# Recurrence gates in four corners of the array, attention heads two by two, and a softmax one projection ahead of its values

## The chip, the cores and the metric

The kernel runs on one core of one Trainium2 chip. The metric is the device time of one execution in microseconds (us). The engines are TensorE (PE; its weight loads are listed as PEld), VectorE (DVE), ScalarE (ACT), GpSimd (POOL) and SyncE (SP). PE writes its results into PSUM banks; ACT and DVE read them from there. DMAs are issued from SP's queue (weights), POOL's and ACT's.

## What is computed

Two blocks in a row on 256 tokens of width 1024, all in 32-bit floats. The first has two layers: dilated attention with spatial gating, then a convolution with stick-breaking attention, each followed by a mixture of 16 experts. The second block has one gated linear recurrence and one neighbourhood attention. What the change touches, cut to its core:

```python
# first block, layer 0: 8 heads of 64, causal, with a relative bias
s = q[h] @ k[h].T * 64**-0.5 + bias[h];  o[h] = softmax(s) @ v[h]

# second block: recurrence over 1024 channels in 16 blocks of 64, both directions
r = sigmoid(block_diag(x, w_r) + b_r)          # gates: 64 x 64 per block
i = sigmoid(block_diag(x, w_i) + b_i)
a = exp(-8 * r * softplus(-lam));  u = sqrt(1 - a*a) * (i * x)
h = associative_scan(a, u)                      # forward and backward

# second block: 16 heads of 64 on a grid of 4 x 64, with a relative bias
o[h] = softmax(q[h] @ k[h].T * 64**-0.5 + nb[h]) @ v[h]
merged = sigmoid(ga) * (y_a @ w_pa) + sigmoid(gb) * ((o * silu(zb)) @ w_pb)
```

## The kernel before

Activations lie with channels on the 128 partitions and the 256 tokens along the free axis, in 8 chunks (`KD`). Every weight tile is 1 MB, loaded by SP into a ring of buffers (`load`, L198); a slot comes free when its projection has used it (`free`). A projection (`proj_ws`, L460) splits a weight tile into a high part `wh` (`split`, L449: ACT at L454, or DVE at L452 where `DVS` says so) and a low part `wl` (DVE, L457). It then does 48 matmuls of 128x128 by 256 columns (L471 to L473), and hands the sums to an evacuation function.

The source order is not the order on the engines. A planner of the language takes the instructions of each engine by their place in the source as a priority, and gives out the first one whose inputs and buffers are ready by its own model of time. The engines then run their queues in that fixed order. So a matmul can stand well ahead of its place in the source, between those of a projection. PSUM banks are taken by `bank(tag, name)`; each of the tags A, B, C and D has two.

**Modulation fill.** `ada_rows` (L347, L351) multiplies one weight tile with a vector, in four column groups of 32. `some_fill` puts such tiles between other work.

**First attention** (L1144 to L1172). For each of four head pairs `hp` and each head `s` in it: two score matmuls into a bank C (L1149, L1150), maximum and bias on DVE (L1153 to L1155), exponentials on ACT (L1157, L1158), normalisation on DVE (L1159 to L1161), three transposes on PE into a bank B (L1164), a copy on ACT (L1166), two value matmuls (L1167, L1168) into the pair's bank D. Then the pair is split into high and low parts (L1169, L1170) and two fill tiles follow.

**Recurrence** (`lru`, L1404 to L1441). It is a generator whose steps stand between the projections `b2_x` 0 to 11 and the first `b2_z`, two after each (`some_lru(LRU)`, L1472, L1482). It takes the 8 chunks of the convolved input `xc` in two halves (`q`) of four. Per chunk: a weight DMA `lw` on POOL's queue (L1412, two buffers), eight gate matmuls of 64 rows by 64 columns on 256 tokens (L1418: two directions `d`, two gates `g`, two blocks `b`), and four sigmoids (L1419, L1420). Block `b` reads partitions 64b to 64b+63 and writes the same partitions. A direction's two gates share a bank B. After the four chunks of a half come exponentials and tanh on ACT, a square root on ACT, and scans on DVE (L1437 to L1440) into `ys`. `ys` is read by the evacuations of `b2_z` 4 to 7.

**zb.** `b2_z` 0 to 3 are evacuated into `zb` (L1481), allocated at L1401, used by the second attention at L1534.

**Second attention** (`attend`, L1505 to L1536). For each of eight pairs: a bias DMA `nb` on POOL's queue (two buffers); per head two score matmuls into a bank C (L1516), maximum and bias on DVE (L1518, L1519), exponentials (L1521), normalisation (L1522 to L1524), four transposes into a bank B (L1528), a copy on ACT (L1530), two value matmuls into the pair's bank D (L1532); then the product with `zb` and the split (L1534 to L1536). The probabilities `sb` have two buffers (pool `lk2`). The loop at L1538 does projection `b2_z` 8+i and then `attend(i)`.

## Time and profile before

| what | us |
|---|---|
| median of three runs | 1213.07 (1211.43 to 1214.85) |
| the profiled execution | 1206.12 |
| its span, first to last instruction | 1204.1 |
| PE busy in the span | 1111.1 (92%) |
| DVE busy | 644.1 (53%) |
| ACT busy | 416.2 (35%) |
| POOL busy | 14.1 (1%) |

The first attention lies at about 108 to 141 us of the span, the first block ends at about 870, the recurrence stands between projections from 884 to 982, and the second attention ends at 1131. The shares are means over stages with different limits, so the rows below are taken stage by stage. Overlapped matmuls are drawn with their full length, so counts and starts of PE rows say more than their busy time.

### The profile page before, as it was taken

Reading aid. Unit: us, or ns where it says so; the run is one execution under the profiler, and the core shown is the slowest. Engines: PE = TensorE matmul, PEld = TensorE weight load, DVE = VectorE, ACT = ScalarE, POOL = GpSimd, SP = SyncE. Lnnn points to the kernel's source line nnn. Section 1 sums busy time; section 2 is a strip of 40 time slices with the busy share of each in tenths; the row PEclk is TensorE's granted clock in tenths of the full one; section 3 lists DMA queues with packets and bytes.
Section 4 is the critical chain, followed back from the end, with each engine's and each line's share of the span. In section 5 each row is a group of like instructions: output and inputs, shape, how many; then the busy total and the mean of one; then the engine's idle time right before and its main releaser. Section 6 shows DMA issues by size and latency. Waiting matters only on the chain. (4 is left out here: it accounts for less than half of the span.)

```text
span 1204.1 us, 20780 instructions
## 1 busy us (share of the span) xinstructions
PE 1111.1 (92%) x8168; PEld 794.1 (66%) x8172; DVE 644.1 (53%) x1488; ACT 416.2 (35%) x802; POOL 14.1 (1%) x32
## 2 busy tenths in 40 slices
PE   5899998999999989999898998899899999999996
PEld 3786575555555469868555554554578889788895
DVE  4665454333333359787623332232598787656665
ACT  2434331111111153365311121111446636445543
POOL 0000000000000000000000000000000000000000
PEclk9899889999999999999999999999899999999998
DMA  9999768999999988568858999998344445544340
GB/s 382 411 401 411 289 255 318 416 410 416 416 418 418 397 309 308 220 247 324 325 207 339 405 420 383 397 409 320 133 175 160 152 142 197 176 153 145 125 173 35
DMA packets 50551, 353.36 MB, mean 293 GB/s; under 512 B 5904, under 2 KB 6288, under 8 KB 8784
## 3 DMA queue, kind: packets, MB, share of 16 engines
q1 hardware_dynamic: 48544, 344.59, 72.9%
q0 software_dynamic: 1552, 6.03, 1.5%
q8 instruction: 104, 1.70, 0.6%
q14 instruction: 63, 0.52, 0.1%
q10 hardware_dynamic: 288, 0.52, 0.1%
HBM read 350.07 MB, written 1.05 MB: 292 GB/s over the span
## 5 line engine op out<-in xcount | busy, mean ns | idle before, releaser
L816 PE MATMUL gu<-ring,xg 128*64 128x256 f32 x1024 | 237.3, 385 | 2.0 <-issue 2.0
L815 PE MATMUL gu<-ring,xg 128*64 128x256 f32 x1024 | 236.9, 385 | 1.7 <-issue 1.6
L471 PE MATMUL pw<-xh,wh 128*128 128x256 f32 x736 | 212.2, 290 | 7.9 <-ACT wh L454 2.6
L457 DVE TENSOR_TENSOR wl<-ring,wh 128x1024 fp32r<-128x1024 f32 x144 | 175.2, 1222 | 71.9 <-ACT wh L454 68.0
L473 PE MATMUL pw<-xh,wl 128*128 128x256 f32 x736 | 210.6, 287 | 2.2 <-DVE wl L457 2.2
L472 PE MATMUL pw<-xl,wh 128*128 128x256 f32 x736 | 209.6, 286 | 0.0
L815 PEld LDWEIGHTS gu<-ring,xg 128*64 128x64 f32 x1024 | 138.1, 138 | 68.6 <-issue 8.4
L454 ACT ACTIVATE wh<-ring 128x1024 fp32r<-128x1024 f32 x114 | 120.0, 1058 | 151.0 <-PE pw L472 80.5
L471 PEld LDWEIGHTS pw<-xh,wh 128*128 128x128 f32 x736 | 141.8, 193 | 19.5 <-issue 11.3
L816 PEld LDWEIGHTS gu<-ring,xg 128*64 128x64 f32 x1024 | 138.2, 138 | 18.9 <-issue 10.3
L473 PEld LDWEIGHTS pw<-xh,wl 128*128 128x128 f32 x736 | 142.2, 193 | 6.0 <-DVE wl L457 3.3
L472 PEld LDWEIGHTS pw<-xl,wh 128*128 128x128 f32 x736 | 142.3, 193 | 1.4 <-DVE mf L1079 0.4
L841 PE MATMUL y<-ring,ht 128*64 128x512 f32 (+1 forms) x576 | 128.1, 563 | 6.6 <-DVE ht L835 5.0
L827 DVE SCALAR_TENSOR_TENSOR hd<-hs,gc,gu 64x256 f32<-64x256 f32 x64 | 30.7, 480 | 162.6 <-ACT hs L826 162.6
L826 ACT ACTIVATE hs<-gu 64x256 f32<-64x256 f32 x66 | 25.0, 379 | 249.0 <-PE gu L816 249.0
L351 PE MATMUL ada<-ring,zc 128*32 128x256 f32 x960 | 71.6, 412 | 14.5 <-DMA ring<-ada 12.2
L841 PEld LDWEIGHTS y<-ring,ht 128*64 128x64 f32 x576 | 39.3, 137 | 53.2 <-issue 33.5
L851 ACT ACTIVATE Y<-yf 64x512 fp32r<-64x512 f32 (+1 forms) x72 | 42.7, 593 | 91.3 <-DVE yf L848 90.4
L852 DVE TENSOR_TENSOR Y<-yf,Y 64x512 fp32r<-64x512 f32 (+1 forms) x72 | 46.2, 642 | 22.8 <-ACT Y L851 21.3
L488 PE MATMUL pt<-wh,xh 128*128 128x512 f32 x144 | 57.3, 399 | 0.8 <-ACT wh L454 0.4
L490 PE MATMUL pt<-wl,xh 128*128 128x512 f32 x144 | 56.3, 392 | 0.5 <-DVE wl L457 0.5
L489 PE MATMUL pt<-wh,xl 128*128 128x512 f32 x144 | 56.3, 391 | 0.0
(390 smaller groups left out, 1518.5 us busy)
## 6 DMA issues: line engine op xcount, KB each, us to landing
ring<-moe SPq DMA_DIRECT2D x192, 1024.0 KB, 9.7
ring<-ada SPq DMA_DIRECT2D x60, 1024.0 KB, 9.8
ring<-b_z SPq DMA_DIRECT2D x24, 1024.0 KB, 4.8
ring<-b_x SPq DMA_DIRECT2D x12, 1024.0 KB, 4.9
ring<-od_q SPq DMA_DIRECT2D x8, 1024.0 KB, 8.9
ring<-ev_q SPq DMA_DIRECT2D x6, 1024.0 KB, 18.0
ring<-ev_v SPq DMA_DIRECT2D x4, 1024.0 KB, 15.3
ring<-ev_o SPq DMA_DIRECT2D x4, 1024.0 KB, 15.3
```

Source lines behind the costliest of these rows:

```text
L351: T.matmul(p[32 * j:32 * j + 32, :256], zc[:, k, 7 - r:39 - r], w[:, k], start=start and k < 4, stop=stop and k >= 4, skip_group_check=True)
L454: S.activation(h, w, AF.Copy)
L457: V.tensor_tensor(l, w, h.bitcast(F32), op=OP.subtract)
L471: T.matmul(p, hk, xh[:, k], start=k == 0, stop=False)
L472: T.matmul(p, hk, xl[:, k], start=False, stop=False)
L473: T.matmul(p, lk, xh[:, k], start=False, stop=k == KD - 1)
L488: T.matmul(p[t], xh[:, k, n], hk, start=k == 0, stop=False)
L489: T.matmul(p[t], xl[:, k, n], hk, start=False, stop=False)
L490: T.matmul(p[t], xh[:, k, n], lk, start=False, stop=k == KD - 1)
L815: T.matmul(p[gs_], xg[:, k], wg[:, k], start=k == 0, stop=k == KD - 1)
L816: T.matmul(p[us], xg[:, k], wu[:, k], start=k == 0, stop=k == KD - 1)
L841: T.matmul(y[64 * h:64 * h + 64, cs], ht[:, k], wd[:, k % 2, h, cs], start=k == 0 and cs.start == 0, stop=k == 3, skip_group_check=cs != s ...
```

## The change

Gates: the input gate's weights (odd places of `lruw`) are swapped between the upper and lower 64 partitions on the host. Two DMAs per chunk on POOL's queue copy the halves of `xc` crosswise into a new tile `xs`, which has the buffer of `zb`; `zb` is allocated later. The recurrence gates go into one bank (tag B, both directions), the input gates into another (tag D); consecutive matmuls lie in the four corners of the array. First attention: the score matmuls of both heads alternate, and the value matmuls of both heads stand together after both softmaxes. Second attention: the same, and `attend` is cut in two: `attend` ends with the probabilities (`sb` with four buffers), `values` begins with the transposes; `attend(i + 1)` stands ahead of projection `b2_z` 8+i, `values(i)` behind it.

```diff
--- before.py
+++ after.py
@@ -153,6 +153,8 @@
     A["b2_o"] = _ts(i["w_o_2"][0])
     A["lruw"] = np.stack([i[n][0].reshape(8, P, 64) for n in ("w_r_f_2", "w_i_f_2", "w_r_b_2", "w_i_b_2")], 1).transpose(2, 0, 1, 3)
 
+    A["lruw"][:, :, 1::2] = np.concatenate([A["lruw"][64:, :, 1::2], A["lruw"][:64, :, 1::2]])
+
     c = np.arange(64)
     c0 = np.clip(c - 8, 0, 48)
     inw = (c[None] >= c0[:, None]) & (c[None] < c0[:, None] + 16)
@@ -1143,15 +1145,17 @@
 
         for hp in range(4):
             po = bank("D", "po")[:, :256]
-            for s in range(2):
-                h, r = 2 * hp + s, slice(64 * s, 64 * s + 64)
-                sc = bank("C", "sc")
-                T.matmul(sc[:, 0:128], qT[r, hp, 0:128], kT[r, hp, 0:128], start=True, stop=True)
-                T.matmul(sc[:, 128:384], qT[r, hp, 128:256], kT[r, hp, 0:256], start=True, stop=True)
+            two = [(2 * hp + s, slice(64 * s, 64 * s + 64)) for s in range(2)]
+            sc = [bank("C", "sc") for s in two]
+            for q, n, k in ((slice(0, 128), slice(0, 128), slice(0, 128)), (slice(128, 256), slice(128, 384), slice(0, 256))):
+                for p, (h, r) in zip(sc, two):
+                    T.matmul(p[:, n], qT[r, hp, q], kT[r, hp, k], start=True, stop=True)
+            pbs = []
+            for p, (h, r) in zip(sc, two):
                 sb = lk().tile([P, 384], F32, name="sb")
                 mx = wk.tile([P, 4], F32, name="mx")
-                V.tensor_tensor_reduce(sb[:, 0:128], sc[:, 0:128], relb[:, h, 128:256], 1.0, -3e38, op0=OP.add, op1=OP.max, accum_out=mx[:, 0:1])
-                V.tensor_tensor_reduce(sb[:, 128:384], sc[:, 128:384], relb[:, h], 1.0, -3e38, op0=OP.add, op1=OP.max, accum_out=mx[:, 1:2])
+                V.tensor_tensor_reduce(sb[:, 0:128], p[:, 0:128], relb[:, h, 128:256], 1.0, -3e38, op0=OP.add, op1=OP.max, accum_out=mx[:, 0:1])
+                V.tensor_tensor_reduce(sb[:, 128:384], p[:, 128:384], relb[:, h], 1.0, -3e38, op0=OP.add, op1=OP.max, accum_out=mx[:, 1:2])
                 V.tensor_scalar(mx[:, 2:4], mx[:, 0:2], -1.0, None, op0=OP.mult)
                 dn = wk.tile([P, 2], F32, name="dn")
                 S.activation(sb[:, 0:128], sb[:, 0:128], AF.Exp, bias=mx[:, 2:3], accum_out=dn[:, 0:1])
@@ -1164,7 +1168,10 @@
                     T.transpose(pt[:, c * P:c * P + P], sb[:, c * P:c * P + P], ident)
                 pb = lk().tile([P, 384], F32, name="pb")
                 S.activation(pb, pt[:, :384], AF.Copy)
+                pbs.append(pb)
+            for pb, (h, r) in zip(pbs, two):
                 T.matmul(po[r], v[:, 0, h * 64:h * 64 + 64], pb[:, 0:256], start=True, stop=False)
+            for pb, (h, r) in zip(pbs, two):
                 T.matmul(po[r, 128:256], v[:, 1, h * 64:h * 64 + 64], pb[:, 256:384], start=False, stop=True)
             S.activation(oh[:, hp], po, AF.Copy)
             V.tensor_tensor(ol[:, hp], po, oh[:, hp].bitcast(F32), op=OP.subtract)
@@ -1398,7 +1405,8 @@
 
         xc = b2.tile([P, KD, NT], F32, name="xc", tag="xc")
         ys = b2.tile([P, KD, NT], F32, name="ys")
-        zb = b2.tile([P, KD, NT], F32, name="zb")
+
+        xs = b2.tile([P, KD, NT], F32, name="xs", tag="zb")
         qT = b2.tile([P, KD, NT], F32, name="qT")
         kT = b2.tile([P, KD, NT], F32, name="kT")
         def lru():
@@ -1410,14 +1418,18 @@
                     c = 4 * q + j
                     lw = bw.tile([P, 4, 64], F32, name="lw")
                     G.dma_start(lw, A["lruw"][:, c])
+                    for b in range(2):
+                        G.dma_start(xs[64 - 64 * b:128 - 64 * b, c], xc[64 * b:64 * b + 64, c])
+
+                    pr, pi = [bank(g, "gate").rearrange("p (d n) -> p d n", d=2) for g in "BD"]
                     for d in range(2):
-                        p = bank("B", "gate").rearrange("p (g n) -> p g n", g=2)
-                        for g in range(2):
-                            for b in range(2):
-                                r = slice(64 * b, 64 * b + 64)
-                                T.matmul(p[r, g], lw[r, 2 * d + g], xc[r, c], start=True, stop=True)
-                        S.activation(R[:, j, d], p[:, 0], AF.Sigmoid, bias=col("brb" if d else "brf", c))
-                        sig = S.activation(I[:, j, d], p[:, 1], AF.Sigmoid, bias=col("bib" if d else "bif", c))
+                        for b in range(2):
+                            r, s = slice(64 * b, 64 * b + 64), slice(64 - 64 * b, 128 - 64 * b)
+                            T.matmul(pr[r, d], lw[r, 2 * d], xc[r, c], start=True, stop=True)
+                            T.matmul(pi[r, d], lw[s, 2 * d + 1], xs[s, c], start=True, stop=True)
+                    for d in range(2):
+                        S.activation(R[:, j, d], pr[:, d], AF.Sigmoid, bias=col("brb" if d else "brf", c))
+                        sig = S.activation(I[:, j, d], pi[:, d], AF.Sigmoid, bias=col("bib" if d else "bif", c))
                     yield
                 for j in range(4):
 
@@ -1476,6 +1488,7 @@
             S.activation(f, p, AF.Tanh, scale=0.5)
             return f
 
+        zb = b2.tile([P, KD, NT], F32, name="zb", tag="zb")
         for i in range(4):
             fill["dve"] = DVS[12 + i]
             proj_ws(("b2_z", i), xh, xl, lambda c, p, i=i: V.scalar_tensor_tensor(zb[:, 2 * i + c], tanh1(p), 1.0, p, op0=OP.add, op1=OP.mult))
@@ -1502,18 +1515,21 @@
         ah = b2.tile([P, KD, NT], F32R, name="ah", tag="lr")
         al = b2.tile([P, KD, NT], F32R, name="al", tag="li")
 
+        probs = {}
+
         def attend(hp):
+
             nb = bw.tile([P, 2, 384], F32, name="nb")
             G.dma_start(nb, A["nb"][:, 2 * hp:2 * hp + 2])
-            po = bank("D", "po")[:, :256]
-            for s in range(2):
-                h, r = 2 * hp + s, slice(64 * s, 64 * s + 64)
-                sc = bank("C", "sc").rearrange("p (t n) -> p t n", t=2)
-                sb = lk().tile([P, 2, 256], F32, name="sb", tag="sb")
+            two = [(2 * hp + s, slice(64 * s, 64 * s + 64)) for s in range(2)]
+            scs = [bank("C", "sc").rearrange("p (t n) -> p t n", t=2) for s in two]
+            for t in range(2):
+                for sc, (h, r) in zip(scs, two):
+                    T.matmul(sc[:, t], qT[r, hp, t * P:t * P + P], kT[r, hp], start=True, stop=True)
+            for s, sc in enumerate(scs):
+                sb = lk().tile([P, 2, 256], F32, name="sb", tag="sb", bufs=4)
                 mx = wk.tile([P, 4], F32, name="mx")
                 dn = wk.tile([P, 2], F32, name="dn")
-                for t in range(2):
-                    T.matmul(sc[:, t], qT[r, hp, t * P:t * P + P], kT[r, hp], start=True, stop=True)
                 for t in range(2):
                     V.tensor_tensor_reduce(sb[:, t], sc[:, t], nb[:, s, 128 - 128 * t:384 - 128 * t], 1.0, -3e38, op0=OP.add, op1=OP.max, accum_out=mx[:, t:t + 1])
                 V.tensor_scalar(mx[:, 2:4], mx[:, 0:2], -1.0, None, op0=OP.mult)
@@ -1522,19 +1538,30 @@
                 V.reciprocal(dn, dn)
                 for t in range(2):
                     V.tensor_scalar(sb[:, t], sb[:, t], dn[:, t:t + 1], None, op0=OP.mult)
+                probs[hp, s] = sb
+
+        def values(hp):
+            po = bank("D", "po")[:, :256]
+            pbs = []
+            for s in range(2):
+                sb = probs[hp, s]
                 pt = bank("B", "ptt").rearrange("p (k n) -> p k n", k=2)
                 for k in range(2):
                     for t in range(2):
                         T.transpose(pt[:, k, t * P:t * P + P], sb[:, t, k * P:k * P + P], ident)
                 pb = lk().tile([P, 2, 256], F32, name="pb", tag="pb")
                 S.activation(pb, pt, AF.Copy)
-                for k in range(2):
-                    T.matmul(po[r], v[:, k, h * 64:h * 64 + 64], pb[:, k], start=k == 0, stop=k == 1)
+                pbs.append(pb)
+            for k in range(2):
+                for s, pb in enumerate(pbs):
+                    h = 2 * hp + s
+                    T.matmul(po[64 * s:64 * s + 64], v[:, k, h * 64:h * 64 + 64], pb[:, k], start=k == 0, stop=k == 1)
             f = lk().tile([P, NT], F32, name="hf")
             V.scalar_tensor_tensor(f, po, 0.5, zb[:, hp], op0=OP.mult, op1=OP.mult)
             S.activation(ah[:, hp], f, AF.Copy)
             V.tensor_tensor(al[:, hp], f, ah[:, hp].bitcast(F32), op=OP.subtract)
 
+        attend(0)
         for i in range(8):
             hold = {}
 
@@ -1543,8 +1570,11 @@
                     hold["s"] = tanh1(p)
                 else:
                     V.scalar_tensor_tensor(mg[:, i], hold["s"], 1.0, p, op0=OP.add, op1=OP.mult)
+
+            if i < 7:
+                attend(i + 1)
             proj_ws(("b2_z", 8 + i), xh, xl, ev, yh, yl)
-            attend(i)
+            values(i)
 
         for i in range(8):
             hold = {}
```

## Rows read from the trace of the kernel before

**Rows 1.** Busy time by stretch, columns as in its first line.

```profile
core 0: us, PE busy (x) PEld busy (x) DVE busy (x) ACT busy (x) POOL busy (x), PEclk, DMA share, GB/s
104.00:133.00 29.00, 29.00 (x234) 15.95 (x234) 19.83 (x74) 16.50 (x47) 0.00 (x0) 1.00 0.93 357
133.00:141.00 8.00, 5.00 (x21) 2.64 (x23) 2.60 (x11) 2.85 (x10) 0.00 (x0) 0.70 0.52 201
...
909.00:932.00 23.00, 21.64 (x174) 20.17 (x173) 22.74 (x37) 14.56 (x31) 0.00 (x0) 1.00 0.39 139
...
954.00:982.00 28.00, 25.27 (x192) 24.01 (x191) 25.59 (x38) 16.25 (x34) 0.00 (x0) 0.95 0.32 114
...
1090.00:1131.00 41.00, 38.06 (x288) 32.38 (x288) 27.53 (x84) 22.93 (x56) 1.60 (x3) 1.00 0.40 136
```

**Rows 2.** Timeline of PE: start, length, engine, line, tiles, count.

```profile
1081.77 1.08 PE L1532 MATMUL po<-pb,v 128*64 128x256 f32 x4
```

**Rows 3.** Timeline of PE in the recurrence.

```profile
900.25 1.07 PE L351 MATMUL ada<-ring,zc 128*32 128x256 f32 x16
901.25 3.97 PE L1418 MATMUL gate<-xc,lw 64*64 64x256 f32 x32
...
905.15 0.38 PE L471 MATMUL pw<-xh,wh 128*128 128x256 f32 x1
...
911.00 0.59 PE L408 MATMUL ada<-e,sel 128*128 128x256 f32 x2
```

**Rows 4.** Timeline of ACT, idle time before it in brackets.

```profile
902.38 0.47 ACT L1419 ACTIVATE lr<-gate,cols 128x256 f32<-128x256 f32 x1 [0.55 <-PE gate L1418]
...
906.13 1.28 ACT L1428 ACT_TABLE_LOAD   x1
```

**Rows 5.** Timeline of PE, waits in the recurrence.

```profile
932.24 0.35 PE L471 MATMUL pw<-xh,wh 128*128 128x256 f32 x1 [1.61 <-DVE wh L452]
...
976.16 0.39 PE L471 MATMUL pw<-xh,wh 128*128 128x256 f32 x1 [0.99 <-DVE zb L1481]
...
979.46 0.58 PE L473 MATMUL pw<-xh,wl 128*128 128x256 f32 x1 [1.74 <-DVE wl L457]
```

**Rows 6.** Line L1412: its instructions (min/median/max ns) and their landing.

```profile
L1412 POOL DMA_DIRECT2D lw<-lruw x8: 536/536/946, 841.8 to 941.6; - x8
...
DMA to landing us min/median/max: 2.8/3.6/5.3
```

**Rows 7.** Line L1524: who waited for it (us, times).

```profile
  PE ptt L1528: 2.9, 4
```

**Rows 8.** Timeline of PE in the second attention.

```profile
1015.52 0.70 PE L1516 MATMUL sc<-kT,qT 64*128 64x256 f32 x2
...
1100.43 1.14 PE L1516 MATMUL sc<-kT,qT 64*128 64x256 f32 x8
...
1107.78 1.29 PE L1532 MATMUL po<-pb,v 128*64 128x256 f32 x8
```

**Rows 9.** Groups by line: count, busy us, mean ns, idle before.

```profile
L1516 PE MATMUL sc<-kT,qT 64*128 64x256 f32 x64 | 11.9, 407 | 0.0
...
L1532 PE MATMUL po<-pb,v 128*64 128x256 f32 x64 | 11.7, 393 | 0.1
```

**Rows 10.** Timeline of PE in the first attention.

```profile
108.40 0.48 PE L1149 MATMUL sc<-kT,qT 64*128 64x128 f32 x2
...
108.72 0.59 PE L1150 MATMUL sc<-kT,qT 64*128 64x256 f32 x2
...
113.27 0.50 PE L1149 MATMUL sc<-kT,qT 64*128 64x128 f32 x4
...
113.59 0.61 PE L1150 MATMUL sc<-kT,qT 64*128 64x256 f32 x4
...
135.13 0.61 PE L1164 MATMUL ptt<-ident,sb 128*128 128x128 f32 x3 [1.78 <-DVE sb L1160]
```

## The prediction

> **What bounds the kernel now.** I read the span by stretches first, for TensorE (PE), VectorE (DVE) and the granted clock [rows 1]. In all three places that the change touches PE is busy almost without a break: 29.00 of 29.00 us in the first attention, 21.64 of 23.00 in the recurrence from 909 on, 38.06 of 41.00 in the last four rounds of the second attention. So PE time that is taken out there is time of the kernel, as long as nothing else is late next. The candidate is DVE in the recurrence: 22.74 of 23.00 us from 909 to 932, 25.59 of 28.00 from 954 to 982. The DMA share is at most 0.40 in the three stretches after 909, and it is 0.93 in the first attention, where PE nevertheless has no wait; so transfers are not what ends these stages. Then I read PE's timeline at the three places, and the waits.
>
> One matmul of two F32 operands is two records of the timeline (64 gate matmuls in the code, 128 records).
>
> **Gates, PE time.** Before, a matmul is 64 rows by 64 columns, and the two that follow each other lie in opposite corners. Four value records of one head, which share their columns and so follow one another, take 1.08 us [rows 2], 0.27 each. The 32 gate records of two chunks take 3.90 us (901.25 to 905.15) [rows 3], 0.12 each: two run side by side, and a chunk costs 1.95. What four side by side cost is not in the gates, but the row just before has it: 16 records of the modulation fill, each on 32 columns, four column groups in turn, take 1.00 us (900.25 to 901.25) [rows 3]. Ends for a chunk: 1.95 (the corners don't run four at a time) and 1.00. I take 1.00, since the fill is the row with the same count, type and 256 columns. So 8 x 0.95 = 7.6 us less PE time.
>
> In those same rows the two corners of a pair write one PSUM bank, each its own half of the partitions, and they overlap. The Trainium skill says the opposite (TensorEngine Tiling (Array Packing), Gotcha 1: PSUM Pressure: "Different row tiles cannot access same PSUM bank simultaneously"). By that rule 32 records would take 32 x 0.27 = 8.6 us, and the new form, which still puts two row tiles into each of its two banks, would gain nothing by it; the trace's 3.90 disagrees for tiles that write different partitions.
>
> **Gates, what is kept of it.** Behind the gates stand ScalarE (ACT) and DVE. Eight sigmoids of 0.47 us, 0.43 apart, follow each pair of chunks: the first starts at 902.38, the ACT table load that follows the last at 906.13 [rows 4], 4.88 after the first matmul. With 1.00 us per chunk and both chunks' banks free it would be about 1.0 + 8 x 0.45 = 4.6. So within a pair the chain ACT, then DVE moves by 0.3 only, plus what the two chunks before them gave (2 x 0.95): about 2.2 of the 3.8 us of each half. The rest turns into a longer PE wait for DVE, of which there are two already: 1.61 us at 932 for a weight copy, 1.74 at 979 for a low part, both queued behind the scans [rows 5]. Kept: 2 x 2.2 = 4.4 us; bounds 0 (DVE takes all) and 7.6.
>
> **Gates, the copies.** Each chunk issues two more DMAs on the POOL queue, behind the chunk's weights. POOL issues the weights' eight in 0.54 to 0.95 us each, and they land 2.8 to 5.3 us after issue [rows 6]; a copy is half their size. 16 x 0.54 = 8.6 us of POOL, which does little else there. The wait to look at is that the weights of chunk c+2 wait on POOL for the gates of chunk c (one buffer of two), and copies queued after them wait too; and PE takes its queue in order, so a gate matmul whose copy is late holds all projection matmuls behind it. The convolved chunks are ready one projection ahead of their gates (the cover: 905.15 to 911.00, 5.85 us for one projection [rows 3]); issue and landing of the copies need 1.1 + 3.6. I take 0.5 us for the first chunk of the half; bounds 0 and +3.6 for each of six chunks. The buffer of the copies is later that of zb: its first write must come after the last gate. It comes at 976 (PE waits 0.99 us for it there, behind the scans [rows 5]), some 25 us after those gates, so this costs nothing unless gates are late by that much.
>
> **Second attention, the stalls.** In the last four pairs PE waits before the transposes for the normalised probabilities, 2.9 us in four waits in all [rows 7]. With the softmax a projection ahead and four probability buffers for two, some 6 us of projection lie in between: -2.9, bound 0. Each softmax now ranks ahead of the next projection's weight splits on DVE and ACT; DVE is busy 27.53 of 41.00 us there [rows 1], so next late is still PE. The bias DMA of each pair is issued one projection earlier too, on a POOL queue with nothing else in it; it hides behind two buffers.
>
> **Second attention, pairs.** In the last four rounds the planner pairs the heads already: eight score records take 1.14 us, eight value records 1.29 [rows 8]. Earlier they come in pieces: two score records alone take 0.70 [rows 8], four value records of one head 1.08 [rows 2]. All 64 score records keep PE busy for 11.9 us and all 64 value records for 11.7 [rows 9]; eight full pairs would take 8 x 1.14 = 9.1 and 8 x 1.29 = 10.3, so 4.2 us are to be had. But the order on PE is the planner's, not the source's: it gives out a matmul when its bank is free, and a pair's two banks come free one after the other. I take 1.5, about a third; bounds: 4.2 less, and with every score matmul alone (32 x 0.70 = 22.4 against 11.9) 10.5 more.
>
> **First attention.** Scores of one head take 0.91 us (108.40 to the end at 109.31), of two heads together 0.93 (113.27 to 114.20) [rows 10]; six of eight heads come alone (the first of them is shown), so 3 x 0.9 = 2.7 are to be had. Value matmuls come alone for six heads too, about as much again (estimate, from the same ratio). The end is a bubble: from 133 to 141 PE is busy for only 5.00 of 8.00 us, its longest wait is 1.78, and the granted clock is 0.70 in 133 to 141 [rows 1, 10], between its two levels, after 1.00 in the stretch before, because head 7's chain follows head 6's. Side by side they would end some 2 us sooner. All of 7 us is the upper bound; the planner's hand-out of banks speaks against it as above. I take 3.0 (half the pairing of scores and values, a little of the tail); bounds +1 and -7. DMA follows: the weights' queue waits for PE's frees here, so what is saved moves the experts' start.
>
> **Sum** against the profiled execution (1206.1, span 1204.1): -4.4 + 0.5 - 2.9 - 1.5 - 3.0 = -11.3, so 1194.8. The median of the runs lies 7.0 above that execution; on it the forecast is 1213.1 - 11.3 = 1202.
>
> **Rivals.**
> A, the forecast: 1202, own range 1195 to 1208.
> B, the recurrence ends with DVE, or four corners run no faster than two, and the gates give nothing: 1213.1 - 2.9 - 1.5 - 3.0 = 1206. For it: 22.74 of 23.00 us [rows 1] and the two waits [rows 5]. Against it: from 954 to 982 DVE still has 2.4 us free [rows 1], and the chain that feeds it begins with sigmoids that wait for gates [rows 4], so it starts earlier too. The Trainium skill's rule on row tiles and a bank (the same section) would give this time as well.
> C, the planner leaves the attentions as they were, since banks and not the source set its order; only gates and copies are left: 1213.1 - 3.9 = 1209.
> D, everything is kept: 7.6 + 2.9 + 4.2 + 7 = 21.7, 1191.
> E, the scores go out one by one: A with +10.5 in place of -1.5, 1214.
> F, slower: the copies. PE stands in its order before gates whose copies have not landed, because POOL queues them behind weights that wait for the gates of two chunks before. Price: 3.6 us of landing for each of six chunks, 21.6; with A's other terms 1202 - 0.5 + 21.6 = 1223. From (11.8 + 3.6) / 6 = 2.6 us of wait per chunk it makes the kernel slower by more than 0.3%. For it: POOL takes its queue in order, and a landing takes up to 5.3 [rows 6]. Against: the convolved chunks are ready a projection ahead [rows 3].
>
> **How the numbers follow.** Chances: A 0.47, B 0.16, C 0.12, D 0.08, E 0.07, F 0.10. A measurement of this kernel tells about 0.3% (3.6 us) from no change: faster is below 1209.4. A gives 0.45 of its 0.47 to faster, B 0.14, C 0.05, D 0.08: 0.72. F is slower: 0.10. The rest, 0.18, is within. The range from 1192 to 1213 leaves out F and about half of D and of E.
>
> **What would show it.** Gates: 16 records of a chunk in about 1.0 us of PE's timeline, not 1.95; if 1.9, four corners don't overlap. B: the waits at 932 and 979 longer by together 3 us or more than the forecast's. F: PE idle right before gate matmuls, ended by the copies' DMA. Second attention: no waits before the transposes, eight score records in one piece; E: many pieces of two. First attention: eight records where there were four, and a shorter gap before the last values. The prediction is wrong if the stretch 884 to 982 doesn't shrink by 2 us at least, or if that from 1051 to 1131 grows.

## The result

The changed kernel takes 1195.02 us (median, 1192.96 to 1197.83) against 1213.05 us for the kernel before on the same chip. The ratio is 0.9858, with a 95% interval from 0.9834 to 0.9882: 17.2 us less, between 14.3 and 20.1 (the two medians lie 18.0 apart). The forecast was 1202, 11.3 us less. The direction and the places were right and the size was too small. Two of the steps behind it were wrong in ways that partly cancel: more of the gates' time was kept than forecast, and the softmax's lead brought less.

The two profiled executions are only 9.9 us apart (1206.12 and 1196.26). The experiments show why that number is not the one to explain: the two expert layers, which the change doesn't touch, took 531.8 us in the profile of before and 537.1 in that of after. In the fourteen profiles of this study they take 529.3 to 540.7 us, with no order by kernel. What can be compared far more closely is a stretch between two instructions that both kernels have: where nothing in it was edited, the first two of the stretches below repeat to 0.5 us (the second but for falls of the clock, which are counted apart) and the third to 0.1. Three stretches are used from here on, each from the start of a numbered matmul record on PE's timeline to the start of the same-numbered record further on (times of before in brackets):

- S1, first attention: from the last transposed-projection block ahead of it (98.6) to the output projection (145.5).
- S2, recurrence: from the first of its projections (874.9) to the fifteenth (986.5).
- S3, second attention: from there to the first projection after it (1137.1).

| kernel | S1 | S2 | S3 | sum |
|---|---|---|---|---|
| before | 46.94 | 111.61 | 150.61 | 309.16 |
| before, profiled again | 47.02 | 113.19 | 150.64 | 310.85 |
| after | 42.88 | 104.15 | 148.09 | 295.11 |

The sum is 14.0 us shorter than in the first profile of before, 15.7 shorter than in the second. That is just under the interval of the measured gain, and in its lower part.

### The profile page after: what moved, and what is told of

Its sections match the earlier page's. It is cut to its first block, busy times and chain, and to the rows that moved or that the text cites. A ratio compares the mean times of both kernels' runs of the same rounds, so it can differ in the third digit from the quotient of the medians.

```text
span 1194.4 us, 20819 instructions
## 1 busy us (share of the span) xinstructions
PE 1103.3 (92%) x8172; PEld 787.8 (66%) x8172; DVE 644.3 (54%) x1488; ACT 415.2 (35%) x802; POOL 23.1 (2%) x48
## 5 line engine op out<-in xcount | busy, mean ns | idle before, releaser
L818 PE MATMUL gu<-ring,xg 128*64 128x256 f32 x1024 | 240.6, 389 | 2.3 <-issue 2.3
L817 PE MATMUL gu<-ring,xg 128*64 128x256 f32 x1024 | 240.3, 389 | 1.9 <-issue 1.8
L817 PEld LDWEIGHTS gu<-ring,xg 128*64 128x64 f32 x1024 | 139.6, 140 | 70.5 <-issue 11.2
L818 PEld LDWEIGHTS gu<-ring,xg 128*64 128x64 f32 x1024 | 139.6, 140 | 18.9 <-issue 10.4
L353 PE MATMUL ada<-ring,zc 128*32 128x256 f32 x960 | 68.9, 393 | 14.0 <-DMA ring<-ada 11.3
## 6 DMA issues: line engine op xcount, KB each, us to landing
ring<-ev_o SPq DMA_DIRECT2D x4, 1024.0 KB, 15.7
```

The costliest lines, as they stand in the source:

```text
L353: T.matmul(p[32 * j:32 * j + 32, :256], zc[:, k, 7 - r:39 - r], w[:, k], start=start and k < 4, stop=stop and k >= 4, skip_group_check=True)
L817: T.matmul(p[gs_], xg[:, k], wg[:, k], start=k == 0, stop=k == KD - 1)
L818: T.matmul(p[us], xg[:, k], wu[:, k], start=k == 0, stop=k == KD - 1)
```

## The profile after

Busy time by stretch, the columns as in the first line; the stretches answer to those of [rows 1], in after's own times.

```profile
core 0: us, PE busy (x) PEld busy (x) DVE busy (x) ACT busy (x) POOL busy (x), PEclk, DMA share, GB/s
104.00:133.00 29.00, 27.86 (x231) 14.26 (x231) 20.39 (x77) 16.93 (x48) 0.00 (x0) 1.00 0.91 358
133.00:141.00 8.00, 6.72 (x64) 4.02 (x64) 2.49 (x11) 2.99 (x10) 0.00 (x0) 1.00 0.82 312
905.00:931.00 26.00, 24.23 (x194) 22.36 (x192) 24.34 (x39) 17.89 (x37) 3.09 (x6) 1.00 0.55 187
950.00:977.00 27.00, 25.59 (x202) 23.98 (x200) 24.38 (x37) 17.54 (x37) 0.00 (x0) 1.00 0.34 118
1090.00:1122.00 32.00, 31.76 (x247) 27.95 (x246) 18.95 (x49) 16.62 (x37) 0.53 (x1) 1.00 0.33 116
```

Two columns matter. PEclk is 1.00 from 133 to 141, where it was 0.70, and 1.00 from 950 to 977, where the stretch of before that answers to it had 0.95. And the recurrence still has PE and DVE both busy for some 90 to 95% of the time: DVE didn't become a longer wait for PE, it came along.

PE's timeline at two chunks of gates (start, length, engine, line, tiles, shape, count):

```profile
900.35 1.07 PE L353 MATMUL ada<-ring,zc 128*32 128x256 f32 x16
901.35 0.43 PE L1428 MATMUL gate<-xc,lw 64*64 64x256 f32 x1
901.35 0.43 PE L1429 MATMUL gate<-xs,lw 64*64 64x256 f32 x1
901.36 0.43 PE L1428 MATMUL gate<-xc,lw 64*64 64x256 f32 x1
901.37 0.43 PE L1429 MATMUL gate<-xs,lw 64*64 64x256 f32 x1
901.61 0.38 PE L1428 MATMUL gate<-xc,lw 64*64 64x256 f32 x1
...
903.24 0.39 PE L473 MATMUL pw<-xh,wh 128*128 128x256 f32 x1
```

Four records start within 0.02 us, the next four 0.26 later. The 32 records of two chunks take 1.89 us (901.35 to 903.24), against 3.90 in [rows 3].

The first of the eight sigmoids behind them, and the ACT table load behind the last, which answer to [rows 4]:

```profile
902.49 0.47 ACT L1431 ACTIVATE lr<-gate,cols 128x256 f32<-128x256 f32 x1 [0.56 <-PE gate L1429]
...
905.53 1.28 ACT L1440 ACT_TABLE_LOAD   x1
```

The table load starts 4.18 us after the first gate, against 4.88 before: the eight sigmoids start 0.36 us apart, without a wait between them.

The waits of PE in the recurrence (in brackets, with what ended them), which answer to [rows 5], and who waited for the copies of line 1422 (us, times) with their landing:

```profile
893.40 0.43 PE L1429 MATMUL gate<-xs,lw 64*64 64x256 f32 x1 [0.66 <-DMA xs<-xc]
910.58 0.40 PE L1428 MATMUL gate<-xc,lw 64*64 64x256 f32 x1 [0.90 <-DMA lw<-lruw]
931.23 0.35 PE L473 MATMUL pw<-xh,wh 128*128 128x256 f32 x1 [1.11 <-DVE wh L454]
971.44 0.38 PE L473 MATMUL pw<-xh,wh 128*128 128x256 f32 x1 [0.75 <-DVE zb L1494]
977.11 0.39 PE L475 MATMUL pw<-xh,wl 128*128 128x256 f32 x1 [0.33 <-DVE wl L459]
```

```profile
L1422 POOL DMA_DIRECT2D xs<-xc x16: 516/523/1051, 885.7 to 914.2; - x16
  PE gate L1429: 0.7, 1
DMA to landing us min/median/max: 1.9/4.3/7.0
```

The three waits for DVE, 1.61, 0.99 and 1.74 before, are 1.11, 0.75 and 0.33, and one of 0.45 for a weight copy is new at 975.64. Two waits for DMA are new, 1.56 us together.

One round of the second attention on PE's timeline, and the end of the first:

```profile
1076.12 1.03 PE L1551 MATMUL ptt<-ident,sb 128*128 128x128 f32 x8
1077.09 0.70 PE L1528 MATMUL sc<-kT,qT 64*128 64x256 f32 x4
1077.85 1.56 PE L1558 MATMUL po<-pb,v 128*64 128x256 f32 x8
1079.34 0.70 PE L1528 MATMUL sc<-kT,qT 64*128 64x256 f32 x4
```

```profile
135.00 0.44 PE L1168 MATMUL ptt<-ident,sb 128*128 128x128 f32 x2 [0.66 <-DVE sb L1165]
...
136.30 1.14 PE L1173 MATMUL po<-pb,vg 128*64 128x256 f32 x3
...
137.81 1.93 PE L353 MATMUL ada<-ring,zc 128*32 128x256 f32 x32
```

The trace lists no wait before the second attention's transposes any more ([rows 7] had four). But the eight scores come in two pieces of four around the values, and the eight value records take 1.56 us instead of 1.29 [rows 8]. In the first attention the longest wait before transposes is 0.66 where it was 1.78 [rows 10].

## The experiments

A ratio is to the kernel before, timed beside it on the same chip; where none is given, there is one execution and its profile. Stretches are S1, S2 and S3 as above. The diffs are cut to what matters, and each is against the kernel with the part that it varies: the gates alone, one attention alone, or the whole change.

**Before again.** No edit.

> The kernel before, unchanged. It measures what a comparison tells from no change, and gives a second profile of it. Theory 1: the first profile of before (1206.1 us) was a fast execution of a kernel whose usual time is 1213, and the 7 us lie in the two expert stretches (193 to 444 and 594 to 875 us of the span), which move from one execution to the next; then this profile shows longer expert stretches, by up to 7 us together, and the same stretches elsewhere to within 0.5 us. Rival: the 7 us are time outside the span or spread evenly. Ratio expected 1.000, within 0.003.

Measured: ratio 1.001 (0.9994 to 1.0025). The span is 1210.7 us, 6.6 over the first profile. Of this the expert layers have 4.7, and 1.5 lies in S2, at one place. So most of the difference lies where the theory put it, but the other stretches don't all agree to 0.5 us. The line where PE's wait for a weight copy ends, and the granted clock of the 9.5 us that follow it, in this profile:

```profile
937.24 0.36 PE L471 MATMUL pw<-xh,wh 128*128 128x256 f32 x1 [1.61 <-DVE wh L452]
```

```profile
937.00:946.50 9.50, 9.26 (x60) 8.30 (x62) 8.13 (x11) 3.62 (x7) 0.87 (x1) 0.82 0.38 128
```

The wait is the 1.61 us of [rows 5]. Here the clock fell after it, to 0.82 in the mean of the stretch, between its two levels of 1.2 and 2.4 GHz; in the first profile it stayed at 1.00. Of the seven profiles of kernels with the old gates and the old operand layout, four show the fall (20.3 us for the two projections there) and three don't (18.8). In the six profiles with four corners, where the wait is 1.1 to 1.5 us, there is none.

**The three parts alone.** Each kernel has only the diff's hunks of one part: gates with copies, first attention, second attention.

> Before with the four-corner gates and their copies alone. Theory 1 (each part takes PE time out of its own stage): the stretch from the first b2_x projection to the last b2_v projection (875 to 1046 in the span) is shorter by 6 to 7 us, ratio 0.995. Rival (what is saved comes back as waits for DVE behind the scans): 2 us or less, ratio 0.998 or more.

> Before with the first attention's heads two by two alone. Theory 1: the stage before the experts ends 4 us earlier, and so does the whole, ratio 0.9965. Rival: the expert stretches, whose DMA share is 1.0, end when their weights have come, and give the 4 us back: ratio 1.000 with an expert stretch longer by what the attention is shorter.

> Before with the second attention's changes alone (heads two by two, softmax a projection ahead, four probability buffers). Theory 1: the four waits before the transposes (2.9 us) go, and the stretch from 1046 to 1131 is shorter by 3 to 4 us, ratio 0.997. Rival: score matmuls in more pieces eat it, ratio 1.000.

| kernel | ratio (95%) | us | S1 | S2 | S3 |
|---|---|---|---|---|---|
| gates alone | 0.9923 (0.9899 to 0.9947) | -9.3 | 47.33 | 103.83 | 151.46 |
| first attention alone | 0.9972 (0.9959 to 0.9984) | -3.4 | 42.87 | 113.42 | 150.58 |
| second attention alone | 0.9986 (0.9970 to 1.0002) | -1.7 | 46.89 | 113.18 | 147.22 |

The product of the ratios is 0.9881, just inside the interval of the whole. By stretch the parts give 6.9, 4.1 and 3.4, together 14.4 against the 14.0 of the whole. So the parts add up, and nothing shows that one needs another. By stretch each theory holds and each rival falls; by time alone the second attention's gain isn't clear of nothing. The gates shorten S2 by 7.8 and lengthen S3 by 0.85, 6.9 us net: in S3, two score records of the second attention now come alone, and the projection around them takes 6.57 us for 5.76. The first attention gives 4.1 in S1. Its S2 is 1.8 longer than in the first profile of before, 1.5 of it because the clock fell after the 2.00 us wait that all these kernels have at the second projection (9.26 us there for 7.79). The second attention gives 3.4 in S3; its S2 has the clock's fall of the run before.

**Gates without the copies.**

```diff
-for b in range(2):
-    G.dma_start(xs[64 - 64 * b:128 - 64 * b, c], xc[64 * b:64 * b + 64, c])
-T.matmul(pi[r, d], lw[s, 2 * d + 1], xs[s, c], ...)
+T.matmul(pi[r, d], lw[s, 2 * d + 1], xc[s, c], ...)
```

> The gate change alone, but without the sixteen crosswise copies: the second pair of corners reads the other half of the untransposed input in place, so half of the input-gate values are computed from the wrong channels; the time of the arithmetic is the same. Theory (the copies cost what the two waits on DMA in the changed kernel show, 0.66 us for a copy and 0.90 us for gate weights queued behind copies): 1.6 us less than the gate change alone, ratio to before about 0.991 against 0.992, and both waits gone from TensorE's rows. Rival 1 (the copies are hidden, other work fills those waits): 0.9923, the same as with copies. Rival 2 (the copies hold more than the two waits, through the order of all that follows): 0.987 or less.

Measured: ratio 0.9916 (0.9885 to 0.9948), which alone can't tell 0.7 per mille from 0.9923. S2 is 102.37 us against 103.83, so the copies cost 1.5 us. This kernel leaves the copies out, so its input gates read the other block's channels. All waits of PE from 880 to 960 in this profile (us in total, times, longest):

```profile
PE pw L473 <- DVE xc L1461: 2.0, 1, 2.0
PE pw L473 <- DVE wh L454: 1.5, 1, 1.5
```

None is before a gate. The theory holds in size; rival 1 falls by the stretch and rival 2 by the time. The second of these waits:

```profile
935.50 0.35 PE L473 MATMUL pw<-xh,wh 128*128 128x256 f32 x1 [1.48 <-DVE wh L454]
```

It ends 53.7 us after the start of S2 (881.8 in this profile). The wait of 1.61 us in [rows 5] is the same one; it ends 57.4 us after that start. So DVE is through with this weight copy 3.6 us earlier, and the wait for it didn't grow.

**Two banks, but two corners.** Both kinds of gates read the same rows of the array again, without copies.

```diff
-T.matmul(pi[r, d], lw[s, 2 * d + 1], xs[s, c], ...)
+T.matmul(pi[r, d], lw[r, 2 * d + 1], xc[r, c], ...)
```

> The two kinds of gate each have their bank and the order of the eight matmuls is that of the change, but both kinds read the same rows of the array, as before, so only two corners are open at a time, and there are no copies. Theory (four corners at once is what shortens the chunk): two chunks take about 3.9 us again instead of 1.9, ratio 1.000 (0.998 to 1.002). Rival (it is the second bank, which lets the sigmoids of one kind start while the other kind is still written): two chunks take well under 3.9 us or the ratio is 0.994 or less.

PE's timeline at two chunks:

```profile
909.90 0.66 PE L1419 MATMUL gate<-xc,lw 64*64 64x256 f32 x4
910.38 0.60 PE L1420 MATMUL gate<-xc,lw 64*64 64x256 f32 x4
...
913.55 0.39 PE L472 MATMUL pw<-xh,wh 128*128 128x256 f32 x1
```

The 32 records take 3.65 us, so four corners are what shortens the chunk. But the ratio is 0.9970 (0.9946 to 0.9994), 0.7 to 6.6 us less than before, and the rival has a share. S2 and S3 together are 262.01 us, and 1.5 of that is a clock fall at the second projection (granted 0.85 there; where no gates lie beside it, such a fall makes it 9.3 us instead of 7.8). Without the fall 260.5, against 262.2 before: 1.7 us come from the second bank and the order that goes with it. PE's waits for DVE behind the scans are 0.7, 0.8 and 0.4 us in this profile, against the three of [rows 5], and the clock doesn't fall behind them. In the kernel before it fell right behind the last one, to 1.2 GHz (columns as in [rows 1]):

```profile
979.30:982.70 3.40, 3.24 (x15) 3.24 (x16) 3.40 (x5) 0.00 (x0) 0.00 (x0) 0.50 0.02 5
```

The matmuls start 0.21 us apart there and 0.12 us apart behind it, so some 1.4 us are lost (estimate from these spacings). This is the 0.95 of [rows 1]. All seven profiles with the old gates have this fall, and none of the seven in which the two kinds of gates have a bank each. How the bank shortens the waits was not tried apart. The step from here to gates without copies is four corners alone: 260.5 to 253.8, 6.7 us of the 7.6 to be had.

Both kinds of gates of a direction in one bank, with four corners, was not tried: two row groups would write the same partitions of one bank at once. So the rule of the Trainium skill (TensorEngine Tiling (Array Packing), Gotcha 1: PSUM Pressure) that different row tiles can't access one bank at the same time stays open for that case. For row tiles that write different partitions of a bank, as both banks have it here, the trace of after disagrees with it: 16 records take 0.94 us. One after another in each of the two banks they would take 8 x 0.27 = 2.2 us, an estimate from [rows 2].

**Copies on SP's queue.** The whole change, with the sixteen copies issued by SP.

```diff
-G.dma_start(xs[64 - 64 * b:128 - 64 * b, c], xc[64 * b:64 * b + 64, c])
+nc.sync.dma_start(xs[64 - 64 * b:128 - 64 * b, c], xc[64 * b:64 * b + 64, c])
```

> The whole change with the sixteen crosswise copies issued from SP's queue instead of POOL's, so that the gate weights no longer stand behind copies. Theory (the copies cost by their place in POOL's queue): the wait of 0.90 us for gate weights goes, the one of 0.66 us for the first copy stays or shrinks, 1194 us, ratio 0.985. Rival (SP's queue carries the projections' weights, and a copy that waits for its input holds them up): TensorE waits for weights between 890 and 950 us by together 3 us or more, 1198 us or more, ratio 0.988 or more.

Measured: ratio 0.9863 (0.9825 to 0.9901), no different from the change. S2 is 102.54 us against 104.15: the whole price of the copies is gone. The waits of PE from 880 to 960:

```profile
PE pw L473 <- DVE xc L1469: 2.0, 1, 2.0
PE pw L473 <- DVE wh L454: 1.1, 1, 1.1
```

No wait for weights, so the rival falls. But S1 is 44.45 us, though PE's instructions there are those of after. The end of the first attention in this profile:

```profile
136.50 1.40 PE L1173 MATMUL po<-pb,vg 128*64 128x256 f32 x3
...
138.68 2.84 PE L353 MATMUL ada<-ring,zc 128*32 128x256 f32 x32
```

```profile
133.00:141.00 8.00, 6.57 (x48) 3.29 (x52) 2.69 (x11) 3.19 (x11) 0.00 (x0) 0.79 0.75 283
```

The same three value records take 1.40 us instead of 1.14, and the 32 fill records behind them 2.84 instead of 1.93, at a granted clock of 0.79. In after the clock stayed at 1.00 through the same gaps. So 1.6 us in the first attention hang on whether the clock falls in its last gaps. Before, it was low for longer, so its share of the 4.1 us may be more: in the last 12 us of S1 it is 0.72 in all eight profiles with the old first attention, 0.86 in this one and 1.00 in the other five with the new one, whole or in part.

**First attention, scores alone two by two.** The values follow each head's own transposes, as before.

```diff
-                pbs.append(pb)
-            for pb, (h, r) in zip(pbs, two):
                 T.matmul(po[r], v[:, 0, h * 64:h * 64 + 64], pb[:, 0:256], start=True, stop=False)
-            for pb, (h, r) in zip(pbs, two):
                 T.matmul(po[r, 128:256], v[:, 1, h * 64:h * 64 + 64], pb[:, 256:384], start=False, stop=True)
```

> Of the first attention's change only the scores two by two; the values follow each head's own transposes, as before. Read by the stretch from the start of the last 24 transposes ahead of the attention (98.6 us in the profile) to the start of the output projection: 46.95 us before, 42.9 us with the whole first part. Theory (the tail of the attention shortens because the last scores no longer come in two pieces after the values of the pair before): 44 us or less, most of the 4.1 us. Rival (issuing the values together brings it): 46 us or more.

S1 is 45.05 us: 1.9 of the 4.1 come with the scores, so neither number was met. The clock stays at 1.00 in the tail of this profile, so the 1.9 us hold what the clock gives back. The tail:

```profile
136.92 0.65 PE L1169 MATMUL po<-pb,vg 128*64 128x256 f32 x2
137.41 0.38 PE L1170 MATMUL po<-pb,vg 128*64 128x128 f32 x2
137.72 0.33 PE L1166 MATMUL ptt<-ident,sb 128*128 128x128 f32 x1
138.69 0.65 PE L1169 MATMUL po<-pb,vg 128*64 128x256 f32 x2 [0.64 <-ACT pb L1168]
```

The last transpose now stands behind the values of the head before it, and its copy out of PSUM is waited for (0.64). Issued together, the values stand behind all transposes, and this wait is gone in after.

**Second attention, the lead alone and the pairs alone.** In the first, scores and values are issued head by head, but scores and softmax one projection ahead. In the second, two by two, but behind their own projection.

```diff
-            for t in range(2):
-                for sc, (h, r) in zip(scs, two):
+            for s, sc in enumerate(scs):
+                h, r = two[s]
+                for t in range(2):
                     T.matmul(sc[:, t], qT[r, hp, t * P:t * P + P], kT[r, hp], start=True, stop=True)
...
-            for k in range(2):
-                for s, pb in enumerate(pbs):
+                for k in range(2):
                     T.matmul(po[64 * s:64 * s + 64], v[:, k, h * 64:h * 64 + 64], pb[:, k], ...)
```

```diff
-            if i < 7:
-                attend(i + 1)
             proj_ws(("b2_z", 8 + i), xh, xl, ev, yh, yl)
+            attend(i)
             values(i)
```

(In the second, the `attend(0)` ahead of the loop is gone too.)

> Of the second attention's change only the lead of one projection: scores, softmax and values of a pair are issued head by head, as before. Read by the stretch from the first of the last two transposed projections' end (start of projection record 1633) to the start of record 2113, 85.6 us before and 81.9 us in the changed kernel. Theory (the lead takes away the waits before the transposes and leaves the last two rounds without scores): 82 us, 3.4 to 4 us less than before, no wait before transposes. Rival (two by two issue brings it): 84.5 us or more.

> Of the second attention's change only the issue two by two, without the lead: a pair's scores and softmax follow their own projection, as before. Same stretch, 85.6 us before. Theory (pairing alone moves nothing, since the eight score records took 1.07 us before already): 85 to 87 us, waits of 0.7 us or more per round before the transposes remain. Rival (pairing is worth the predicted 1.5 us by itself): 84.5 us or less.

By the stretch named there (from record 1633) the lead alone takes 86.2 us and the pairs alone 84.3, against 85.6 before and 81.9 with both. But that stretch was badly chosen: with the lead, scores move across its start. By S3, which holds both sides, the lead alone gives 149.01, the pairs alone 148.93, both 147.22, against 150.61: 1.6, 1.7 and 3.4 us less. Half each, and they add up. The theory that the lead brings it all falls, and so does the theory that the pairs alone move nothing. A round with the lead alone, and a wait of the pairs alone:

```profile
1084.54 1.04 PE L1538 MATMUL ptt<-ident,sb 128*128 128x128 f32 x8
1085.51 1.13 PE L1516 MATMUL sc<-kT,qT 64*128 64x256 f32 x4
1086.56 1.26 PE L1543 MATMUL po<-pb,v 128*64 128x256 f32 x8
1087.76 1.13 PE L1516 MATMUL sc<-kT,qT 64*128 64x256 f32 x4
```

```profile
1106.16 0.30 PE L1538 MATMUL ptt<-ident,sb 128*128 128x128 f32 x1 [0.59 <-DVE sb L1527]
```

With the lead the waits are gone, but the planner hands out the scores in two pieces of four. Head by head such a piece is one head and takes 1.13 us; two by two it is half of both heads and takes 0.70. So the lead alone gives back 2 x 1.13 - 1.14 = 1.1 us of each of the last four rounds, and the pairs undo most of it. All scores and all transposes of the second attention with the lead alone (count, busy us, mean ns, idle before, as in [rows 9]), and all its transposes in the kernel before:

```profile
L1516 PE MATMUL sc<-kT,qT 64*128 64x256 f32 x64 | 16.3, 407 | 0.0
...
L1538 PE MATMUL ptt<-ident,sb 128*128 128x128 f32 x64 | 8.3, 273 | 0.0
```

```profile
L1528 PE MATMUL ptt<-ident,sb 128*128 128x128 f32 x64 | 10.4, 276 | 2.9 <-DVE sb L1524 2.9
```

The lead takes away 2.9 us of waits and 2.1 us of transposes, which now come eight at a time, and adds 4.4 us of scores; with 0.5 us less for the values that makes 1.1 of its 1.6 us. With the pairs alone, four waits stay, 2.2 us together: 0.7 of the 1.7 us are shorter waits, and scores and values have 0.9 (11.4 and 11.3 us for the 11.9 and 11.7 of [rows 9]). The eight value records take 1.26 us head by head and 1.56 two by two; scores two by two with values head by head were not tried.

**Two probability buffers instead of four.** The whole change, with `bufs=4` taken off the probabilities.

> The whole change with two buffers for the second attention's probabilities instead of four, so that a pair's softmax can't be written before the transposes of the pair before it have read theirs. Theory (being one projection ahead is what takes away the waits before the transposes): the waits come back, the stretch from the ninth gating projection to the last is 3 to 7 us longer than in the changed kernel, and the time is 1198 to 1202 us, ratio to before 0.988 to 0.991. Rival (two by two issue alone brought the gain, or the softmax is early enough anyway): 1195 us, ratio 0.986, no wait before the transposes above 0.3 us.

Measured: ratio 0.9861 (0.9826 to 0.9896), the same as the change. S3 is 147.27 us, 0.8 shorter than after, with no wait before the transposes: the theory falls and the rival holds. A round:

```profile
1069.83 1.04 PE L1551 MATMUL ptt<-ident,sb 128*128 128x128 f32 x8
...
1071.56 1.56 PE L1558 MATMUL po<-pb,v 128*64 128x256 f32 x8
1073.05 1.13 PE L1528 MATMUL sc<-kT,qT 64*128 64x256 f32 x8
```

The planner now gives the eight scores out in one piece of 1.13 us, where after needs 2 x 0.70, and a piece of the projection lies between the transposes and the values. That later free buffers hold the scores back is argued, not shown. S2 is 104.14 us, as in after, by another way: here the clock fell at the second projection (0.82), and PE waits for no copy, though the copies are on POOL's queue. The copies start no earlier, 10.3 us into S2 against 10.0 in after, but the slowed PE comes to the first gate 17.3 us into S2 instead of 15.5. So the price of the copies and that of this fall overlap. The span of this profile is 1187.6 us, 6.8 less than after, but 7.8 of that lie in the expert layers, which have nothing to do with it; the median of the runs is 1196.4.

**Both variants together.**

> The whole change with the crosswise copies on SP's queue and two probability buffers instead of four: the two variants that each shortened their stretch. Theory (the two add up): the recurrence's stretch 7.9 us and the second attention's 3.9 us shorter than before, against 6.3 and 3.7 in the changed kernel; 1193 us, ratio to before 0.984. Rival (the two shift pieces of work onto each other): stretches no shorter than in the changed kernel, ratio 0.986 or more.

Measured: ratio 0.9861 (0.9840 to 0.9882), 1196.75 us. The stretches add up as the theory has it: S1 42.88, S2 102.38, S3 147.27, together 292.53 against 295.11 of after. (The expectation's 7.9 and 3.9 us belong to stretches that meet at record 1633; by those it is 8.7 and 3.9.) The theory's time, 1193 us, was not met. The time doesn't show these 2.6 us: 0.9861 against 0.9858, with intervals of 0.2% to either side. So this is a kernel with shorter stages that hasn't been shown to be faster.

## Why the prediction was right, and where it was wrong

| step | forecast | by stretch | part alone, timed (95%) |
|---|---|---|---|
| gates and copies | -3.9 | -6.9 | -9.3 (-12.2 to -6.4) |
| second attention | -4.4 | -3.4 | -1.7 (-3.6 to +0.2) |
| first attention | -3.0 | -4.1 | -3.4 (-5.0 to -1.9) |
| whole | -11.3 | -14.0 | -17.2 (-20.1 to -14.3) |

**Gates, PE time: right.** 1.00 us per chunk was taken from the fill's row; 0.94 was measured. Rival B is out: four corners do run faster than two, and waits for DVE didn't take the gain.

**Gates, what is kept: wrong, and the main miss.** The step said that DVE is late next and that 3.2 of the 7.6 us turn into longer waits for it. The waits became shorter, and 6.7 us of four corners were kept, plus 1.7 from the second bank and its order, which the prediction gave nothing. The error was in the reasoning on the chain of sigmoids. It let that chain move by 0.3 us within a pair of chunks; it moved by 0.7 (4.18 us for 4.88), because the sigmoids come 0.36 us apart and not 0.45. And it treated the DVE time of the stretch as a block behind the chain. A stretch in which DVE is 22.74 of 23.00 us busy [rows 1] was read as a stretch with DVE at its limit. But that work is fed by PE through the gates, so it starts earlier when they do: without the copies, the weight copy that PE waits for comes 3.6 us earlier, nearly all of the 3.8 us of the first half, where the step kept 2.2. The prediction says this itself, as an argument against B, and didn't let it into the sum. The 0.95 of the granted clock from 954 to 982 stands in [rows 1] too, and the prediction makes nothing of it: its fall behind the 1.74 us wait cost some 1.4 us (estimate above), which the new gates take away.

**The copies: mechanism right, size low.** F's mechanism is there: PE idle before a gate, ended by a copy, and once by weights queued behind copies. It cost 1.5 us, not 0.5, and not 21.6: it struck twice, not for each of six chunks.

**Second attention, the stalls: wrong as a step.** The waits are gone as forecast, but the lead alone gave 1.6, not 2.9, because the scores that it sends ahead come in pieces (4.4 us more); that the transposes come together (2.1 us less) wasn't forecast either. That the order on PE is the planner's was known; it was applied to the pairs only. **The pairs: right in size, in part by luck**, -1.7 against -1.5, not by the full pairs that were costed. Alone, 0.7 of it are shorter waits. With the lead, the pairs make the pieces cheaper and the values dearer (1.56 against 1.29), and the sign that was named, eight score records in one piece, didn't come. Four buffers, to which the step gave the softmax's room, are not what brings it.

**First attention: right in place, 1.1 us low.** About half came with the scores alone, half with the values issued together. The sum left out that the clock, 0.70 there before, would stay up: 1.6 us in the one profile of the new form in which it fell.

**Base.** The forecast was made against the profiled execution and carried to the median with +7.0. This held: the expert layers were fast in that execution. What it left out is the clock's fall behind the 1.61 us wait in S2, which the first profile doesn't have and four of seven profiles with the old gates do: 0.9 us in the mean (an estimate, 4/7 of 1.5) that the new gates also take away. The stretches and this make 14.9 of the measured 17.2 us. The rest is inside the interval; nothing here shows a further cause.

**Which rival.** By the time alone, 1195 us is nearer to D's 1191 than to A's 1202, and at the very end of A's own range. The stretches tell them apart: D has 7 us in the first attention and 4.2 in the pairs, and they gave 4.1 and 1.7.

## What to carry to other kernels

An engine that is busy all through a stretch isn't its limit while the engine ahead of it still feeds it: ask whether its first instruction would start earlier. When a row of the trace shows the clock below full, give the fall behind a wait a price of its own, beside the wait. Where single profiles differ in parts that no edit touched, compare stretches between the same instructions, and choose them wide enough that nothing moved across their ends. When work is sent ahead of its place, look at the pieces in which it then comes: eight scores took 1.13 us in one piece, 1.40 in two of both heads, 2.26 in two of one head each.

## What the hardware showed unexpectedly

Waits of the same length did and didn't cost clock: after the same 1.61 us wait the granted clock was 1.00 in three profiles and 0.82 to 0.84 in four, 1.5 us each time. After the 2.00 us wait at the second projection it fell in four of fourteen, 1.5 us again. After the two waits of 0.99 and 1.74 us at the end of the recurrence, 1.6 us apart, it fell in all seven profiles with the old gates, some 1.4 us each time (estimate). In the first attention's tail the same instructions took 1.6 us more in the profile in which it fell. So a gap of PE that is shortened can give back more than its length, but not in every execution.

A copy of half a chunk within the chip (64 x 256 F32, 64 KB) took POOL 0.52 us to issue and landed 1.9 to 7.0 us later, 4.3 in the median. The sixteen of them on POOL's queue cost 1.5 us of PE time; on SP's queue, among the streamed weights, none that the trace shows.
